# Stick-breaking attention layer: one copy of queries, keys and values out of PSUM, sums of squares and output halves off VectorE, keys converted first

## The chip, the core and the metric

The kernel runs on one core of a Trainium2 chip. The core has five engines that run their own instruction streams and meet at semaphores: TensorE (PE in the profile, its weight loads PEld), VectorE (DVE), ScalarE (ACT), GpSimd (POOL) and SyncE (SP), which issues the DMAs. The metric is the device time of one execution in microseconds (us), taken as the median of several runs. Lower is better.

## The reference

One step of a two-layer decoder trunk, in float32, for 1024 prompt rows and 64 sample rows (8 sequences of 8). Layer 0 is gated linear attention; layer 1, which the change touches, is stick-breaking attention with 16 heads of 64 columns:

```
u = rms_norm(x) @ w_in_b                      # 1024 -> 4 * 1024: q, k, v, gate
q, k = rms_norm(q per head) * qn, rms_norm(k per head) * kn
z = q . k / 8 + bias
a[t, s] = sigmoid(z[t, s]) * prod over s < j < t of (1 - sigmoid(z[t, j])),  s < t
y = x + ((a @ v) * silu(gate)) @ w_out_b      # k and v rows are outputs as well
```

## The kernel before

Matrix products run as float32r in three passes: each operand is split into a high part (a rounded copy) and a low part (the rest), and high·high, high·low and low·high are added up in PSUM. The rounded copy is an ACT activation, or a VectorE cast, and the rest is a subtraction on VectorE or POOL; for the weights these are `whi` (L219 on ACT, L221 on DVE) and `wlo` (L222).

Layer 1 runs over eight pairs of heads. For a pair PE makes nine blocks of rows (eight of 128 prompt rows, one of the 64 sample rows): `columns` multiplies the block's normalized rows by 384 columns of the weights (q, k and v of two heads) into a PSUM bank named `acc`, with 24 matmuls (L293). After every second block `gates` computes the gate columns for 256 rows, transposed, into an `acc` bank too (L315). The attention of the previous step runs between these matmuls: per step m (four to a pair) and head it goes over blocks of 256 keys. One unit is: logits `z` (four matmuls, L881), two sigmoids `om` and `A` on ACT (L884, L885), two running products `run` on DVE (scans, L904 on the diagonal, L907 elsewhere), a product `A` times `run` (L912, L915), transposes of `A` on PE (L928), their split into `aT` high (ACT L930) and low (DVE L931), and the matmuls with the values (L942). POOL hands the last column of one running product to the next (L899).

The steps around the change, by their functions:

- `qk_sums` takes a block's `acc` bank: ACT squares q and k of four heads (L799) and copies v out (L801), DVE adds the squares up per head (L802), POOL raises the mean to the power -0.5 (L804). For the sample block the bank is first copied to an SBUF tile `xr` (`whole_rows`).
- `qk_scale` multiplies q and k, still in the `acc` bank, by that factor (DVE L810); only then is the bank free for the next `columns` or `gates`. POOL makes the key output (L812); `v_parts` (L819, L820) splits the values.
- `qk_p` takes the blocks two by two: PE transposes q and k into a `tr` bank (L829), ACT and DVE split them into `qh`, `ql` and `kc`. The `tr` bank also serves the transposes of `A`.
- `gate_b` adds, at the end of a step, the two partial products of each head from the `o` bank (L952, L953) and multiplies by the gate (POOL L954); `store_b` sends the result to DRAM, or for the last pair to `H`, the input of the last projection.

PSUM has eight banks here, two each of `acc`, `tr`, `z` and `o`. PE's order is written out: every matmul has a due time (`at(...)`), and PE takes them by due time. The order on the other engines is made when the program is built, by a scheduler that plans with its own costs; each engine then works strictly in its order. Where ACT and DVE read the same PSUM bank, the built program puts a wait between them, so that one is done before the other starts.

Of the kernel before, what the change touches and what calls it, by code (L numbers as in the profile page):

```python
# [9 lines left out]
F32 = mybir.dt.float32  # L10
# [21 lines left out]
EPS = 1e-6  # L32
# [44 lines left out]
def tile_hybrid_decoder(ctx, tc, x_prompt, x_sample, state_gla, cache_k, cache_v, page_table,  # L77
# [16 lines left out]


    FIRST0, FIRST, FIRST5, RAW0 = 0.9, 1.5, 6, 0.9
    ACT_FROM, WHI, DLO = 90, 6, 3

    GAIN, CONSTS, SUP, LATE = -64.9, 2.5, 0.9, 9
    LAT, LAT0, LQ, LK = .7, 1.2, 1.4, 1.3  # L100
# [33 lines left out]
    def rows(t):  # L134
        return 128 if t < NP else NS
# [633 lines left out]
    def l1_consts():  # L769
        opened("keep")  # L770
        opened("at1")
        qn = K1["qn"] = const.tile([128, 1], F32, name="qn")
        for j in range(2):
            nc.sync.dma_start(qn[j * 64:(j + 1) * 64], cut(qnorm_b, 0, [[1, 64], [1, 1]]))
        nc.vector.tensor_scalar(qn, qn, DH ** -0.5, None, op0=OP.mult)
        bcast(K1.setdefault("kn", const.tile([128, DH], F32, name="kn")), knorm_b, 0, DH)
        knt = K1["knt"] = const.tile([128, 1], F32, name="knt")
        for j in range(2):
            nc.sync.dma_start(knt[j * 64:(j + 1) * 64], cut(knorm_b, 0, [[1, 64], [1, 1]]))
        bias = K1["bias"] = const.tile([128, 2, SH], F32, name="bias")  # L780
        bcast(bias[:, 0], sb_bias, 0, SH)
        nc.vector.tensor_scalar(bias[:, 1], bias[:, 0], -1.0, None, op0=OP.mult)
        gains = K1["gains"] = const.tile([128, 1], F32, name="gains")
        nc.vector.tensor_mul(gains, qn, knt)
        for name in ("qTs", "kTs", "gTs"):
            K1[name] = sb("keep", name, [128, PAIRS, NS], F32, 1)

        K1["sq"] = sb("at1", "sq", [128, 4, DH + 1], F32, 1)
        nc.gpsimd.memset(K1["sq"][:, :, DH:], EPS)

    def qk_sums(st, p, t):
        n = rows(t)
        if t == NP:
            whole_rows(st, "at1", 384)
        ps = st["ps"]
        sq = K1["sq"]
        q4 = ps[:n, :256].rearrange("p (h d) -> p h d", d=DH)
        ms = small.tile([128, 4], F32, name="ms4")
        nc.scalar.activation(sq[:n, :, :DH], q4, AF.Square, scale=1.0 / 8.0)  # L799
        st["v"] = sb("at1", "v", [128, 128])  # L800
        nc.scalar.activation(st["v"][:n], ps[:n, 256:384], AF.Copy)  # L801
        nc.vector.tensor_reduce(ms[:n], sq[:n], axis=AX.X, op=OP.add)  # L802
        st["rs"] = small.tile([128, 4], F32, name="rs4")
        nc.gpsimd.tensor_tensor(st["rs"][:n], ms[:n], half_exp[:n], op=OP.pow)  # L804

    def qk_scale(st, p, t):
        n, ps, rs = rows(t), st["ps"], st["rs"]
        q4 = ps[:n, :256].rearrange("p (h d) -> p h d", d=DH)
        qk = st["qk"] = sb("at1", "qk", [128, 4, DH], F32, 4)
        nc.vector.tensor_mul(qk[:n], q4, rs[:n, :, None].to_broadcast([n, 4, DH]))  # L810
        st["kout"] = sb("at1", "kout", [128, 2, DH])
        nc.gpsimd.tensor_mul(st["kout"][:n], qk[:n, 2:], K1["kn"][:n, None].to_broadcast([n, 2, DH]))  # L812

# [23 lines left out]
    def qk_p(sts, pair):  # L837

        tr = psum.tile([128, 4, 128], F32, name="tr")
        for x, st in enumerate(sts):
            turn_qk(st, 128, tr, (x, 2 + x))
        tr = tr.rearrange("p a s -> p (a s)")
        qp, kp, g = tr[:, :256], tr[:, 256:], K1["gains"]
        qh, kc = sb("at2", "qh", [128, 2, 256], F32R, NQ), sb("at2", "kc", [128, 2, 256], F32R, NKV)
        ql = K1["ql"][K1["turn"] % NQ]
        K1["turn"] += 1
        pair["q"].append((qh, ql))
        pair["k"].append(kc)  # L850
        up, dn = slice(0, 64), slice(64, 128)
        for dst, j, src in ((up, 0, up), (dn, 1, dn), (dn, 0, up), (up, 1, dn)):
            nc.scalar.activation(qh[dst, j], qp[src], AF.Copy, scale=g[src])  # L853
        nc.scalar.activation(kc[up, 0], kp[up], AF.Copy)
        nc.scalar.activation(kc[dn, 1], kp[dn], AF.Copy)
        nc.vector.scalar_tensor_tensor(ql[up, 0], qp[up], g[up], qh[up, 0], op0=OP.mult, op1=OP.subtract)
        nc.vector.scalar_tensor_tensor(ql[dn, 1], qp[dn], g[dn], qh[dn, 1], op0=OP.mult, op1=OP.subtract)
        nc.vector.tensor_sub(kc[dn, 0], kp[up], kc[up, 0])  # L858
        nc.vector.tensor_sub(kc[up, 1], kp[dn], kc[dn, 1])  # L859

    def gate_t(st, p, m, pair):
        ps, gt = st["ps"], sb("at1", "gt", [128, 256], F32, NG)
# [83 lines left out]
    def gate_b(q, pair, p, m):  # L946
        po = q["po"]
        sh, og = sb("at2", "sh", [128, 256], F32, 1), sb("at2", "og", [128, 256], F32, 2)
        q["og"] = og
        for j in range(2):  # L950
            main, other = slice(64 * j, 64 * j + 64), slice(64 - 64 * j, 128 - 64 * j)
            nc.scalar.activation(sh[main], po[other, j], AF.Copy)  # L952
            nc.vector.tensor_add(og[main], po[main, j], sh[main])  # L953
        nc.gpsimd.tensor_mul(og, og, pair["g"][m])  # L954

    def tps(m):
# [297 lines left out]
```

## Time and profile before

| | |
|---|---|
| median of three runs | 1348.04 us (1348.0 to 1350.47) |
| the profiled execution, its own time | 1349.09 us |
| its span, first to last instruction | 1347.4 us |
| granted TensorE clock | 1.00 over the whole span |
| busy, share of the span | PE 94%, PEld 84%, DVE 75%, ACT 53%, POOL 38% |
| layer 1's attention, 540 to 1210 us | eight pairs, one every 85 us |

A matmul's busy time overlaps the next one's, since they are pipelined: a stream of 384-column matmuls starts one every 0.17 to 0.18 us, though each is listed with 0.35 us. ACT's instructions overlap a little as well. "Idle before" and the list of waits count gaps that were ended by a semaphore, with the instruction that set it.

### The profile page before, as it was taken

The numbers are of one execution on the slowest core, as the hardware profiler recorded it, in microseconds if no ns is written. First come the engines' busy times: TensorE is split into PE (matmuls) and PEld (weight loads), VectorE is DVE, ScalarE is ACT, GpSimd is POOL, SyncE is SP. The second block draws the span as 40 slices with busy tenths as digits, with TensorE's granted clock in tenths as the row PEclk, the third lists the DMA queues.
The fourth block names the chain that finished last, engine by engine and source line by source line (L and its number), as shares of the span: only waits on it lengthen the run. The fifth ranks groups of instructions, "written<-read, shape, count | busy, mean of one in ns | idle before, by whom it ended". The sixth has DMA issues, their size and how long they took to land.

```text
span 1347.4 us, 23358 instructions
## 1 busy us (share of the span) xinstructions
PE 1269.9 (94%) x8025; PEld 1128.5 (84%) x8025; DVE 1011.1 (75%) x2047; ACT 708.4 (53%) x1640; POOL 515.5 (38%) x847
## 2 busy tenths in 40 slices
PE   6899999999999999989989999899998999999998
PEld 5788888888887787889989899898898998978665
DVE  7857858759565357698898988988889889896543
ACT  6446245254352034566666766667667677763221
POOL 6222323223222215363453734646446464443000
PEclk9999999999999999999999999999999999999999
DMA  6311402403327443020120200202002022134862
GB/s 193 91 41 44 135 20 59 124 17 100 121 90 240 135 137 117 20 73 27 34 71 23 71 27 28 79 23 70 28 28 77 21 78 86 33 124 152 316 204 79
DMA packets 118456, 115.80 MB, mean 86 GB/s; under 512 B 11002, under 2 KB 97922, under 8 KB 118338
## 3 DMA queue, kind: packets, MB, share of 16 engines
q1 hardware_dynamic: 118338, 114.31, 27.5%
q8 instruction: 64, 1.05, 0.3%
q14 instruction: 54, 0.44, 0.1%
HBM read 83.61 MB, written 30.67 MB: 85 GB/s over the span
## 4 chain that ended last, share of the span: by engine, by line
PE 56%; DVE 25%; ACT 7%; issue 5%; POOL 4%; DMA 3%; SPq 0%; DVEq 0%; POOLq 0%; ACTq 0%
PE acc L293 33%; PE acc L315 6%; DVE run L907 4%; PE z L881 3%; PE tr L928 3%; PE o L942 2%; DVE aT L931 2%; DVE whi L221 2%; ACT qh L853 2%; DVE qk L810 1%; POOL rs L804 1%; DVE A L912 1%; DVE A L915 1%; PE o L544 1%; DVE run L904 1%
## 5 line engine op out<-in xcount | busy, mean ns | idle before, releaser
L293 PE MATMUL acc<-whi,h 128*128 128x512 f32 (+1 forms) x1728 | 538.1, 374 | 9.3 <-DVE qk L810 6.2
L293 PEld LDWEIGHTS acc<-whi,h 128*128 128x128 f32 x1728 | 312.8, 189 | 40.3 <-ACT sh L952 3.8
L293 PE MATMUL acc<-wlo,h 128*128 128x512 f32 (+1 forms) x864 | 322.6, 373 | 3.9 <-DVE wlo L222 2.5
L315 PE MATMUL acc<-h,whi 128*128 128x256 f32 (+5 forms) x832 | 191.7, 316 | 19.1 <-DVE qk L810 8.7
L222 POOL TENSOR_TENSOR wlo<-wr,whi 128x512 fp32r<-128x512 f32 x98 | 144.4, 1478 | 127.4 <-DVE whi L221 92.5
L293 PEld LDWEIGHTS acc<-wlo,h 128*128 128x128 f32 x864 | 162.5, 188 | 22.1 <-DVE wlo L222 3.2
L315 PEld LDWEIGHTS acc<-h,whi 128*128 128x128 f32 (+2 forms) x832 | 137.8, 185 | 26.2 <-issue 10.6
L907 DVE TENSOR_TENSOR_SCAN run<-om,run 128x256 f32<-128x256 f32 x192 | 141.8, 779 | 15.6 <-ACT om L884 15.1
L930 ACT ACTIVATE aT<-tr 128x512 fp32r<-128x512 f32 (+1 forms) x160 | 89.0, 556 | 82.8 <-PE tr L928 80.9
L884 ACT ACTIVATE om<-z,bias 128x512 f32<-128x512 f32 (+1 forms) x160 | 103.1, 644 | 48.3 <-PE z L881 39.6
L293 PE MATMUL acc<-w,h 128*128 128x384 f32 (+1 forms) x480 | 122.0, 365 | 0.8 <-DVE qk L810 0.8
L315 PE MATMUL acc<-h,wlo 128*128 128x256 f32 (+2 forms) x392 | 122.2, 312 | 0.3 <-POOL wlo L222 0.3
L931 DVE TENSOR_TENSOR aT<-tr,aT 128x512 fp32r<-128x512 f32 (+1 forms) x160 | 100.9, 631 | 9.7 <-ACT aT L930 7.4
L928 PE MATMUL tr<-ident,A 128*128 128x128 f32 x576 | 90.0, 274 | 18.6 <-DVE kc L859 8.4
L885 ACT ACTIVATE A<-z,bias 128x512 f32<-128x512 f32 (+1 forms) x160 | 102.4, 640 | 0.0
L942 PE MATMUL o<-aT,v 128*128 128x256 f32 (+1 forms) x640 | 98.1, 274 | 0.0
L928 PEld LDWEIGHTS tr<-ident,A 128*128 128x128 f32 x576 | 68.9, 140 | 34.0 <-ACT sq L799 9.0
L942 PEld LDWEIGHTS o<-aT,v 128*128 128x128 f32 x640 | 94.4, 188 | 1.7 <-DVE aT L931 1.0
L804 POOL TENSOR_TENSOR rs<-ms,half_exp 128x4 f32<-128x4 f32 (+1 forms) x72 | 86.2, 1198 | 21.3 <-DVE ms L802 18.8
L881 PE MATMUL z<-kc,qh 128*128 128x256 f32 x320 | 84.4, 286 | 7.2 <-DVE kc L858 7.2
L293 PEld LDWEIGHTS acc<-w,h 128*128 128x128 f32 x480 | 83.2, 189 | 6.3 <-issue 0.8
L899 POOL COPY run<-run 128x2 f32<-128x2 f32 x96 | 32.8, 342 | 135.7 <-DVE run L907 78.1
(273 smaller groups left out, 2488.7 us busy)
## 6 DMA issues: line engine op xcount, KB each, us to landing
wr<-in_w_in_b_dram SPq DMA_DIRECT2D x64, 256.0 KB, 3.0
wr<-in_w_in_a_dram SPq DMA_DIRECT2D x32, 256.0 KB, 2.9
kp<-in_cache_k_dram SPq DMA_DIRECT2D x16, 512.0 KB, 4.6
vp<-in_cache_v_dram SPq DMA_DIRECT2D x16, 512.0 KB, 4.9
o_d<-og SPq DMA_DIRECT2D x60, 128.0 KB, 1.8
x<-in_x_prompt_dram SPq DMA_DIRECT2D x8, 512.0 KB, 5.2
wr<-in_w_in_a_dram SPq DMA_DIRECT2D x32, 128.0 KB, 3.9
n<-in_state_gla_dram SPq DMA_DIRECT2D x8, 512.0 KB, 4.2
```

Source lines behind the costliest of these rows:

```text
L222: engine.tensor_sub(e.lo[:, :m], raw[:, :m], e.hi[:, :m])
L293: nc.tensor.matmul(st["ps"][:x.shape[1], :n], x, (w[k].hi if part == 0 else w[k].lo)[:, :n], start=first, stop=last)
L315: nc.tensor.matmul(st[key][:x.shape[1], :n], x, y, start=first, stop=last)
L804: nc.gpsimd.tensor_tensor(st["rs"][:n], ms[:n], half_exp[:n], op=OP.pow)
L881: nc.tensor.matmul(out, lhs, rhs, start=x == 0, stop=x == len(mm) - 1)
L884: nc.scalar.activation(u["om"][:, v0:], z[:, v0:], AF.Sigmoid, scale=-1.0, bias=K1["bias"][:, 1, hd:hd + 1])
L885: nc.scalar.activation(u["A"][:, v0:], z[:, v0:], AF.Sigmoid, bias=K1["bias"][:, 0, hd:hd + 1])
L907: nc.vector.tensor_tensor_scan(run[:, a, n - 1::-1], rev, rev, before[:, a, 0:1], op0=OP.mult, op1=OP.bypass)
L928: nc.tensor.transpose(tr[:, x], u["A"][:, col:col + 128], ident)
L930: nc.scalar.activation(hi[:, v0:], tr[:, v0:], AF.Copy)
L931: nc.vector.tensor_sub(lo[:, v0:], tr[:, v0:], hi[:, v0:])
L942: nc.tensor.matmul(q["po"][:, j, q0:], vs, part[:, x * 256 + q0:(x + 1) * 256], start=first and n == 0, stop=last and n == 3)
```

## The change

It is in layer 1, and in which engine rounds some of its weights.

- `qk_sums`: ACT copies the whole `acc` bank, 384 columns, to an SBUF tile `qkv` (L797). The four heads' squares are taken from that tile, one activation per head with the sum as an accumulated output (L801, four times). The sum on DVE is gone. POOL's power takes a helper with two instructions, an addition of the small constant and the power (L248, L249).
- `qk_scale` multiplies in place in `qkv` (DVE L807), reading two SBUF tensors, where it read PSUM and one SBUF tensor.
- `qk_p`: the same splits in another order, keys first, each high part followed by its low part. The second copies of the high queries are made from the SBUF tile (L858, L859).
- `gate_b`: ACT copies both halves out of the `o` bank (four copies, L952 and L953), POOL adds them (L954).
- `WHI` goes from 6 to 8: of each eight weight tiles whose first use comes after a due time of 90, all are rounded on ACT (L219), not six.

```diff
-    ACT_FROM, WHI, DLO = 90, 6, 3
+    ACT_FROM, WHI, DLO = 90, 8, 3
...
-        K1["sq"] = sb("at1", "sq", [128, 4, DH + 1], F32, 1)
-        nc.gpsimd.memset(K1["sq"][:, :, DH:], EPS)
+        K1["sq"] = sb("at1", "sq", [128, 4, DH], F32, 1)
...
         ps = st["ps"]
         sq = K1["sq"]
-        q4 = ps[:n, :256].rearrange("p (h d) -> p h d", d=DH)
+
+        all3 = sb("at1", "qkv", [128, 384], F32, 4)
+        nc.scalar.activation(all3[:n], ps[:n, :384], AF.Copy)
+        st["qk"], st["v"] = all3[:, :256].rearrange("p (h d) -> p h d", d=DH), all3[:, 256:]
         ms = small.tile([128, 4], F32, name="ms4")
-        nc.scalar.activation(sq[:n, :, :DH], q4, AF.Square, scale=1.0 / 8.0)
-        st["v"] = sb("at1", "v", [128, 128])
-        nc.scalar.activation(st["v"][:n], ps[:n, 256:384], AF.Copy)
-        nc.vector.tensor_reduce(ms[:n], sq[:n], axis=AX.X, op=OP.add)
+        for h in range(4):
+            nc.scalar.activation(sq[:n, h], st["qk"][:n][:, h], AF.Square, scale=1.0 / 8.0, accum_out=ms[:n, h:h + 1])
         st["rs"] = small.tile([128, 4], F32, name="rs4")
-        nc.gpsimd.tensor_tensor(st["rs"][:n], ms[:n], half_exp[:n], op=OP.pow)
+        rsqrt(st["rs"][:n], ms[:n])
 
     def qk_scale(st, p, t):
-        n, ps, rs = rows(t), st["ps"], st["rs"]
-        q4 = ps[:n, :256].rearrange("p (h d) -> p h d", d=DH)
-        qk = st["qk"] = sb("at1", "qk", [128, 4, DH], F32, 4)
-        nc.vector.tensor_mul(qk[:n], q4, rs[:n, :, None].to_broadcast([n, 4, DH]))
+        n, rs, qk = rows(t), st["rs"], st["qk"]
+        nc.vector.tensor_mul(qk[:n], qk[:n], rs[:n, :, None].to_broadcast([n, 4, DH]))
...
         up, dn = slice(0, 64), slice(64, 128)
-        for dst, j, src in ((up, 0, up), (dn, 1, dn), (dn, 0, up), (up, 1, dn)):
-            nc.scalar.activation(qh[dst, j], qp[src], AF.Copy, scale=g[src])
         nc.scalar.activation(kc[up, 0], kp[up], AF.Copy)
+        nc.vector.tensor_sub(kc[dn, 0], kp[up], kc[up, 0])
         nc.scalar.activation(kc[dn, 1], kp[dn], AF.Copy)
+        nc.vector.tensor_sub(kc[up, 1], kp[dn], kc[dn, 1])
+        nc.scalar.activation(qh[up, 0], qp[up], AF.Copy, scale=g[up])
         nc.vector.scalar_tensor_tensor(ql[up, 0], qp[up], g[up], qh[up, 0], op0=OP.mult, op1=OP.subtract)
+        nc.scalar.activation(qh[dn, 1], qp[dn], AF.Copy, scale=g[dn])
         nc.vector.scalar_tensor_tensor(ql[dn, 1], qp[dn], g[dn], qh[dn, 1], op0=OP.mult, op1=OP.subtract)
-        nc.vector.tensor_sub(kc[dn, 0], kp[up], kc[up, 0])
-        nc.vector.tensor_sub(kc[up, 1], kp[dn], kc[dn, 1])
+
+        nc.scalar.activation(qh[dn, 0], qh[up, 0], AF.Copy)
+        nc.scalar.activation(qh[up, 1], qh[dn, 1], AF.Copy)
...
         q["og"] = og
         for j in range(2):
             main, other = slice(64 * j, 64 * j + 64), slice(64 - 64 * j, 128 - 64 * j)
+            nc.scalar.activation(og[main], po[main, j], AF.Copy)
             nc.scalar.activation(sh[main], po[other, j], AF.Copy)
-            nc.vector.tensor_add(og[main], po[main, j], sh[main])
+        nc.gpsimd.tensor_add(og, og, sh)
         nc.gpsimd.tensor_mul(og, og, pair["g"][m])
```

PE's order does not change: its matmuls stand in the same sequence. What changes there are waits. At the gates of step 0 of the fifth pair (`acc` banks with their numbers) PE has before:

```order
L293 MATMUL acc_10235<-w0103_10058,h1_81 128x384
L293 MATMUL acc_10235<-whi_10071,h0_80 128x384
L293 MATMUL acc_10235<-wlo_10072,h0_80 128x384
L293 MATMUL acc_10235<-whi_10071,h1_81 128x384
L315 MATMUL acc_10327<-h0_80,whi_8903 128x256 [waits DVE_49,PE_49]
L315 MATMUL acc_10327<-h1_81,whi_8903 128x256
```

And with the change:

```order
L293 MATMUL acc_10320<-w0103_10141,h1_81 128x384
L293 MATMUL acc_10320<-whi_10154,h0_80 128x384
L293 MATMUL acc_10320<-wlo_10155,h0_80 128x384
L293 MATMUL acc_10320<-whi_10154,h1_81 128x384
L315 MATMUL acc_10414<-h0_80,whi_8964 128x256
L315 MATMUL acc_10414<-h1_81,whi_8964 128x256
```

The first gate matmul's wait on DVE (for L810, which freed its bank) is gone; an earlier wait of PE covers what remains.

On ACT, at the third conversion of the fourth pair (`kc` and `qh` are the converted keys and queries, `aT` the transposed weights of an attention unit, `sq` the squares), the order before is:

```order
L885 ACTIVATE A<-z,bias 128x512
L853 ACTIVATE qh<-tr,gains 64x256 [waits PE_49]
L853 ACTIVATE qh<-tr,gains 64x256 x3
L854 ACTIVATE kc<-tr 64x256
L855 ACTIVATE kc<-tr 64x256
L930 ACTIVATE aT_9855<-tr 128x384 [waits PE_49,Activation_49]
L799 ACTIVATE sq<-acc 128x4x64 [waits PE_49]
L801 ACTIVATE v<-acc 128x128 [waits DMAHW7_49]
```

With the change:

```order
L885 ACTIVATE A<-z,bias 128x512
L849 ACTIVATE kc<-tr 64x256 [waits PE_49]
L851 ACTIVATE kc<-tr 64x256 [waits DVE_49]
L930 ACTIVATE aT_9933<-tr 128x384 [waits PE_49,Activation_49]
L797 ACTIVATE qkv<-acc 128x384 [waits DMAHW3_49,PE_49]
L853 ACTIVATE qh<-tr,gains 64x256 [waits DVE_49]
L801 ACTIVATE sq,ms_9950<-qkv 128x64 [waits Activation_49]
L801 ACTIVATE sq,ms_9950<-qkv 128x64 x3
L858 ACTIVATE qh<-qh 64x256 [waits Activation_49]
L855 ACTIVATE qh<-tr,gains 64x256 [waits DVE_49]
L859 ACTIVATE qh<-qh 64x256 [waits Activation_49]
```

Six activations in a row have become a sequence with three waits on DVE in it, and with other work between them.

On DVE, at the same conversion (`ql` is the low part of the queries), before:

```order
L915 TENSOR_TENSOR A<-A,run 128x512 [waits DVE_49,Activation_49,Pool_49]
L856 SCALAR_TENSOR_TENSOR ql_5789<-tr,gains,qh 64x256 [waits PE_49,Activation_49]
L857 SCALAR_TENSOR_TENSOR ql_5789<-tr,gains,qh 64x256
L858 TENSOR_TENSOR kc<-tr,kc 64x256
L859 TENSOR_TENSOR kc<-tr,kc 64x256
L931 TENSOR_TENSOR aT_9856<-tr,aT_9855 128x384 [waits Activation_49]
```

With the change:

```order
L915 TENSOR_TENSOR A<-A,run 128x512 [waits DVE_49,Activation_49,Pool_49]
L850 TENSOR_TENSOR kc<-tr,kc 64x256 [waits Activation_49]
L852 TENSOR_TENSOR kc<-tr,kc 64x256 [waits Activation_49]
L931 TENSOR_TENSOR aT_9934<-tr,aT_9933 128x384 [waits Activation_49]
L854 SCALAR_TENSOR_TENSOR ql_5791<-tr,gains,qh 64x256 [waits Activation_49]
L856 SCALAR_TENSOR_TENSOR ql_5791<-tr,gains,qh 64x256 [waits Activation_49]
L807 TENSOR_TENSOR qkv<-qkv,rs_9955 128x256 [waits DMAHW3_49,Pool_49]
```

One wait on ACT has become four, each for one activation, and the scaling L807 stands in this stretch with a wait on POOL.

## Rows read from the trace of the kernel before

**Rows 1.** Layer 1: length, busy us of PE, PEld, DVE, ACT, POOL; clock, DMA

```profile
540.00:1210.00 670.00, 625.87 (x4335) 595.43 (x4336) 581.12 (x1114) 453.57 (x965) 337.65 (x570) 1.00 0.17 51
```

**Rows 2.** The chain that ended last, by engine, whole span

```profile
PE 56%; DVE 25%; ACT 7%; issue 5%; POOL 4%; DMA 3%; SPq 0%; DVEq 0%; POOLq 0%; ACTq 0%
```

**Rows 3.** PE's waits, 540 to 1210 us: total, times, longest

```profile
PE acc L315 <- DVE qk L810: 10.4, 7, 1.7
PE tr L928 <- DVE kc L859: 8.4, 6, 2.4
PE z L881 <- DVE kc L858: 7.2, 10, 1.4
PE acc L293 <- DVE qk L810: 7.0, 14, 1.2
PE tr L928 <- ACT sq L799: 4.5, 7, 1.0
```

**Rows 4.** Timeline, 852 to 860 us: start, length, instruction [idle before <- releaser]

```profile
852.21 0.39 ACT L799 ACTIVATE sq<-acc 128x256 f32<-128x256 f32 x1 [1.25 <-DVE ms L802]
...
854.55 0.42 DVE L802 TENSOR_REDUCE ms<-sq 128x4 f32<-128x260 f32 x1
...
856.17 1.38 POOL L804 TENSOR_TENSOR rs<-ms,half_exp 128x4 f32<-128x4 f32 x1
...
859.54 0.41 DVE L810 TENSOR_TENSOR qk<-acc,rs 128x256 f32<-128x256 f32 x1
...
860.10 0.36 PE L315 MATMUL acc<-h,whi 128*128 128x256 f32 x1 [1.72 <-DVE qk L810]
```

**Rows 5.** Groups by shape, 540 to 1210 us: count | busy us, mean ns | idle

```profile
L930 ACT ACTIVATE aT<-tr 128x384 fp32r<-128x384 f32 x63 | 30.9, 491 | 43.7 <-PE tr L928 43.3
L953 DVE TENSOR_TENSOR og<-o,sh 64x256 f32<-64x256 f32 x62 | 25.7, 415 | 1.7
L952 ACT ACTIVATE sh<-o 64x256 f32<-64x256 f32 x62 | 23.5, 379 | 35.9 <-DVE og L953 34.9
L801 ACT ACTIVATE v<-acc 128x128 f32<-128x128 f32 x61 | 17.4, 285 | 0.0
L221 DVE CAST whi<-wr 128x512 fp32r<-128x512 f32 x14 | 9.4, 669 | 0.0
```

**Rows 6.** Groups by shape on POOL, whole span

```profile
L954 POOL TENSOR_TENSOR og<-og,gt 128x256 f32<-128x256 f32 x32 | 26.6, 830 | 37.9 <-DVE og L953 37.9
L248 POOL TENSOR_SCALAR ms<-ms 128x1 f32<-128x1 f32 x32 | 8.5, 267 | 119.2 <-ACT og L645 118.8
```

**Rows 7.** ACT's timeline in layer 0, 173 to 176 us

```profile
173.81 0.40 ACT L561 ACTIVATE qh<-g 128x64 fp32r<-128x64 f32 x2
174.24 0.39 ACT L645 ACTIVATE og<-o 128x256 f32<-128x256 f32 x1
174.52 0.20 ACT L645 ACTIVATION_READ_ACCUMULATOR og<-o 128x1 f32 x1
174.61 0.38 ACT L529 ACTIVATE gt<-acc 128x256 f32<-128x256 f32 x1
```

**Rows 8.** Timeline, 822.5 to 829.5 us: the fourth pair's third conversion

```profile
822.59 0.60 PE L829 MATMUL tr<-ident,qk 128*128 128x128 f32 x4
...
823.23 1.92 ACT L853 ACTIVATE qh<-tr,gains 64x256 fp32r<-64x256 f32 x4
...
824.62 0.49 PE L928 MATMUL tr<-ident,A 128*128 128x128 f32 x3
...
826.97 0.42 DVE L858 TENSOR_TENSOR kc<-tr,kc 64x256 fp32r<-64x256 f32 x1
...
827.53 0.36 PE L881 MATMUL z<-kc,qh 128*128 128x256 f32 x1 [0.56 <-DVE kc L858]
```

**Rows 9.** DVE's and POOL's timelines, 854 to 857 us

```profile
854.88 1.18 DVE L810 TENSOR_TENSOR qk<-xr,rs 64x256 f32<-64x256 f32 x1
...
854.38 1.39 POOL L222 TENSOR_TENSOR wlo<-wr,whi 128x512 fp32r<-128x512 f32 x1
```

## Prediction

> **What bounds the kernel now.** I read the busy times of layer 1 first, since the change is only there: of 670 us PE is busy for 626, DVE 581, ACT 454 and POOL 338 [rows 1]. So PE sets the pace, and what a change of waits can give back is at most its idle time, 670 - 625.9 = 44 us. Next the chain of waits: 56% of the span on PE, 25% on DVE, only 7% on ACT and 4% on POOL [rows 2]. PE's fixed order stops now and then, and mostly DVE lets it go on. Then the list of PE's waits, to see for what: five rows make 37.5 of the 44 us [rows 3]. They are of two families. In the first, a new product needs an `acc` bank that L810 has not yet read: 10.4 + 7.0 = 17.4 us. In the second, PE waits for the conversion of keys and queries, either for the first logits (7.2 us, L858) or for the `tr` bank that the conversion still reads (8.4 us, L859, and 4.5 us which the view puts down to L799, at the first conversion of each pair). Last I read one wait of each family in the timeline [rows 4, 8].
>
> **The change, part by part.**
>
> *The copy out of PSUM.* The timeline shows what held the bank: the block is complete at 852.2, ACT squares it at once, but DVE adds up at 854.55, POOL's power starts at 856.17, L810 at 859.54, and PE, which had come to its gates at 860.10 - 1.72 = 858.4, goes on at 860.10 [rows 4]. With the change the bank is free when the copy L797 ends. For its time I take ACT's copy of the same shape out of PSUM, 0.49 us [rows 5]. The bank would be free near 852.7, some 5 us before PE wants it, which covers an ACT that is late. So the first family goes: -17.4 us. What is late next is the scaling itself: L807 still waits for POOL, and on DVE scans or a product of `A` stand behind it, for which PE's transposes wait. If that gives back all of the gate waits, the L315 row, -7.0 us is left; this is the other end.
>
> *The conversion, in another order.* Six activations and then four DVE operations become eight steps in turn, because the engines may not read the bank together; L851, L853 and L855 each wait for DVE, and behind them on ACT stand the copies L930 and the sigmoids L884 that PE needs. For the first logits I add up the new order at the third conversion, where PE waited 0.56 us before [rows 8]. The transposes end at 823.2. L849 0.38, L850 0.42, L851 0.38 bring 824.4 (before, the same activations and subtractions took 0.38 and 0.42 [rows 5, 8]); L930 must wait for its transposes, which end at 825.1, and takes 0.49; then L797 0.49, L853 0.48 (a quarter of 1.92 [rows 8]), the four squares 0.96 (below), L858 0.4: 827.9. With hand-offs it is 828.0, against 827.53. The logits of one head need no more than this, as its low query part L854 is done by then. So 0.5 us is lost per pair, times 8: +4 us. The ends: -7.2 us if the wait vanishes, and, if two DVE steps take 1.18 us, as L810 beside POOL [rows 9], in place of 0.42, 0.5 + 2 x 0.76 = 2.0 us per pair, +16 us.
>
> The wait for the `tr` bank, 8.4 + 4.5 = 12.9 us, does not stay as it is: by the built program's semaphores the transposes that waited for L859 now take the other bank at most conversions and wait for the L931 that read it. That operation comes early in the conversion, but with one bank left the units follow one another more strictly. I take half, -6.5 us; the ends are -12.9 and, were the wait twice as long, +12.9.
>
> *Loads.* DVE loses 72 sums of 0.42 us [rows 4], 64 additions of 0.415 and 16 casts of 0.67 [rows 5]: 30.2 + 26.6 + 10.7 = 67.5 us. L807 is another instruction than L810: it reads two SBUF tensors. Out of PSUM L810 takes 0.41 us [rows 4]; its sample form, which reads two SBUF tensors as well, took 1.18 us while POOL ran, and ended 0.29 us after POOL's instruction [rows 9]. So 64 of them cost between nothing and 64 x 0.77 = 49 us more; POOL is busy half of the time [rows 1], so I take 25. DVE then has 581 - 67.5 + 25 = 539 us.
>
> ACT gains most. A 64-column activation adds 0.15 us (two in 0.40, one alone 0.25), and an accumulated output 0.09 (the next instruction starts that long after the read of the accumulator) [rows 7]: 0.24 per square, 0.96 for four. With the copy, 0.52, that is 1.48 us, against 0.39 + 0.285 less 0.1 of overlap for L799 and L801 [rows 4, 5]: +0.9, times 72, +65 us. At most, with nothing overlapped, a square costs 0.25 + 0.20, and this is +125. To it come 64 more copies in `gate_b` of 0.38 us [rows 5], +24, and the 16 casts, +11. ACT has 454 + 100 = 554 us, at most 614. POOL gains 72 additions of about 0.27 and 32 sums of 0.83 us [rows 6], 19 + 27: 384 us.
>
> All three stay below PE's 626 and lie beside it, so the loads themselves cost nothing in my sum; what they cost if that cover is too thin is in the rivals. In `gate_b` the work from the `o` bank to the result grows from two copies and two additions in turn (1.6 us) to four copies and a sum on POOL (2.35 us). Only the last step of the last pair has the next stage waiting for it: +0.8 us.
>
> *Sum.* The profiled execution's own time is 1349.1 us (span 1347.4), 1 us above the median of the runs: 1349.1 - 17.4 + 4.0 - 6.5 + 0.8 = 1330.0, and 1329 on the scale of the median.
>
> **Rivals.**
>
> *Hand-offs between ACT and DVE become the bound (slower).* The place is `qk_p`: ACT, now at 83 to 92% load, stands still at L851, L853 and L855 until DVE has finished scans queued ahead of its part. The price is the upper end of both conversion terms: 12.9 + 16 + 0.8 - 17.4 = +12.3, or 1361 us. It decides from the point where a pair loses more than the 2.2 us (17.4 over 8) that the free banks give it: logits of the third conversion later than 4.9 + 2.2 = 7.1 us after its transposes start, against 4.9 before. For it speak the three new waits. Against it: before the change ACT took up the conversion 0.04 us after the transposes [rows 8], so it had no queue.
>
> *VectorE is not lightened (no change).* L807 pays 49 us, and POOL's 46 us more hold DVE's scans and products, which read two SBUF tensors too, for two fifths of that time, 18 us: DVE is at 581 - 67.5 + 67 = 581 again. The chain's 25% on DVE stays, and what the banks give PE returns as waits for `A` and `aT`: 1349 us. The 1.18 us of [rows 9] speak for it; against it, that the two waits of L810 needed no faster DVE to go, only an earlier release. The Trainium skill has this as a rule (GPSIMD Engine Reference, section Key points): GpSimd shares its SBUF interfaces with VectorE and contends with VectorE instructions that have two SBUF inputs. The trace agrees, with 1.18 against 0.41 us. By that rule this rival is the outcome if POOL is nearly always at work when L807 starts.
>
> *Everything goes (faster still).* If both families vanish, 17.4 + 12.9 + 7.2 = 37.5 us of the 44 are won: 1312 us. An ACT without a queue and a DVE with 40 us less speak for it; that PE would then run 40 us ahead of engines at over 80% load speaks against it.
>
> **How the numbers follow.** The forecast (1312 to 1346 us by its own terms) has a chance of 0.50, the last rival 0.14, no change 0.14, slower 0.22. A measurement of this kernel can tell 0.2%, 2.7 us, from no change. The rival without change lies within that with 0.08, on the faster side with 0.05 and on the slower with 0.01. Faster: 0.50 + 0.14 + 0.05 = 0.69; same 0.08; slower 0.22 + 0.01 = 0.23. The range reaches from just below the lowest sum, 1310, into the slower rival, 1357.
>
> **What would show it.** Right: the rows for `acc` that name L810 are gone from PE's waits, with none for L807 and only tenths for L797 in their place; DVE near 540 us and ACT near 550 in layer 1; squares of 0.25 us, starting 0.24 apart; L807 between 0.4 and 1.2 us, long where POOL is busy; L881 of a third conversion some 5.4 us after its transposes start. The forecast is wrong if PE's idle time in layer 1 does not fall by some 20 us: with ACT rows (`aT`, `kc`, `qh`) on top of PE's waits the first rival holds, with `A` or `aT` on DVE and L807 near 1.2 us the second.

## The result, and the profile after

The changed kernel takes 1359.74 us (median of four runs, 1357.2 to 1363.18) against 1348.02 us before (median of four): a ratio of 1.0083, 95% interval 1.0067 to 1.0098. It is slower by 0.8%; the forecast was 1329 us, with a range of 1310 to 1357. The profiled execution's own time is 1363.18 us, 14.1 above the profiled one of before, and 3.4 above the median of its runs, which matters when its numbers are added up.

The busy times of layer 1 after, columns as in [rows 1]; the window is 10 us longer, since the same work now takes about that much more:

```profile
540.00:1220.00 680.00, 632.54 (x4341) 608.11 (x4340) 530.37 (x971) 532.21 (x1537) 378.74 (x673) 0.98 0.17 50
```

The engines are loaded as intended: DVE fell from 581 to 530 us, ACT rose from 454 to 532. But PE's idle time did not fall from its 44 us. It is 680 - 632.5 = 47.5, and PE's own busy time grew by 6.7 us at a mean clock of 0.98 where it was 1.00. So of 10 us lost here 3.4 are idle and 6.7 are slower matmuls; the other 4 are lost mostly at layer 1's first transposes and, 3.4 of them, in the sample stage.

The chain that ended last, after (before: [rows 2]):

```profile
PE 49%; DVE 22%; ACT 14%; POOL 7%; issue 5%; DMA 2%; DVEq 0%; SPq 0%; POOLq 0%; ACTq 0%
```

ACT's share doubled, PE's fell by 7 points. PE's waits after, the same view and window as [rows 3]:

```profile
PE tr L928 <- DVE aT L931: 19.0, 19, 1.9
PE z L881 <- ACT qh L858: 16.8, 8, 2.7
PE tr L928 <- DVE A L915: 4.8, 7, 1.2
PE o L942 <- DVE aT L931: 4.2, 4, 1.2
PE z L881 <- DVE ql L854: 2.7, 1, 2.7
```

Both `acc` rows, 17.4 us, are gone and nothing named L797 or L807 took their place. In their stead stand 19.5 us for first logits (7.2 before), 23.8 for the `tr` bank (12.9 before in the two rows of [rows 3], 17.5 in all its rows) and 4.2 for `aT` at L942. The timeline shows how, at the third conversion of the fourth pair, the place of [rows 8]; here it is the pair before, where nothing differs but the start (start, length, instruction, [idle before <- releaser]):

```profile
737.27 0.60 PE L826 MATMUL tr<-ident,qkv 128*128 128x128 f32 x4
...
737.95 0.38 ACT L849 ACTIVATE kc<-tr 64x256 fp32r<-64x256 f32 x1
...
738.24 1.74 DVE L907 TENSOR_TENSOR_SCAN run<-om,run 128x256 f32<-128x256 f32 x2
...
740.11 0.69 DVE L915 TENSOR_TENSOR A<-A,run 128x512 f32<-128x512 f32 x1
...
740.84 0.42 DVE L850 TENSOR_TENSOR kc<-tr,kc 64x256 fp32r<-64x256 f32 x1
...
741.29 0.38 ACT L851 ACTIVATE kc<-tr 64x256 fp32r<-64x256 f32 x1 [2.96 <-DVE kc L850]
741.69 0.49 ACT L930 ACTIVATE aT<-tr 128x384 fp32r<-128x384 f32 x1
...
742.08 0.48 ACT L797 ACTIVATE qkv<-acc 128x384 f32<-128x384 f32 x1
...
742.45 0.46 ACT L853 ACTIVATE qh<-tr,gains 64x256 fp32r<-64x256 f32 x1
...
742.81 0.25 ACT L801 ACTIVATE sq<-qkv 128x64 f32<-128x64 f32 x1
...
743.89 0.41 ACT L858 ACTIVATE qh<-qh 64x256 fp32r<-64x256 f32 x1
...
744.36 0.38 PE L881 MATMUL z<-kc,qh 128*128 128x256 f32 x1 [2.68 <-ACT qh L858]
```

ACT begins at once, and then stands for 2.96 us, because DVE's half L850 is queued behind a pair of scans and a product. The copy and the four squares come between L851 and L858. The logits start 7.1 us after the transposes; before it was 4.9.

What the clock did there, by windows (columns as in [rows 1]; the third number from the end is the granted clock):

```profile
740.00:745.30 5.30, 2.62 (x18) 2.29 (x18) 3.04 (x6) 3.88 (x16) 2.14 (x6) 1.00 0.05 16
745.30:748.70 3.40, 3.40 (x15) 3.31 (x15) 2.96 (x7) 1.63 (x3) 0.65 (x2) 0.50 0.08 24
748.70:752.10 3.40, 3.40 (x25) 3.40 (x25) 0.84 (x2) 1.57 (x3) 0.00 (x0) 1.00 0.00 0
```

PE was busy for half of 5.3 us; then the granted clock is 0.50, the lower of its two levels, 1.2 GHz, for 3.4 us with PE full, and 15 matmuls are done where the next 3.4 us at 2.4 GHz do 25.

PE's order is the same before and after, so each matmul can be set beside its twin. By this the changed kernel loses 3.7 us at that conversion, 2.1 at the logits and 1.6 under the low clock, but wins most of that back within the pair: it is 1.3 us behind the kernel before at the second pair's first conversion, level at the fourth's third, 4.3 behind at the seventh's first and 5.8 at the last pair's first. The other 8.3 of 14.1 us are lost from there on, where the clock falls for 6.8 us in the last pair and once more in the sample stage.

### The profile page after: what moved, and what is told of

It reads as the page before. It is cut to its first block, busy times and chain, and to the rows that moved or that the text cites. A ratio compares the mean times of both kernels' runs of the same rounds, so it can differ in the third digit from the quotient of the medians.

```text
span 1361.5 us, 23619 instructions
## 1 busy us (share of the span) xinstructions
PE 1276.3 (94%) x8025; PEld 1140.7 (84%) x8025; DVE 957.0 (70%) x1895; ACT 788.6 (58%) x2224; POOL 558.5 (41%) x950
## 4 chain that ended last, share of the span: by engine, by line
PE 49%; DVE 22%; ACT 14%; POOL 7%; issue 5%; DMA 2%; DVEq 0%; SPq 0%; POOLq 0%; ACTq 0%
PE acc L293 31%; PE acc L315 5%; DVE run L907 5%; POOL rs L249 2%; ACT sq L801 2%; PE z L881 2%; DVE A L915 2%; PE o L942 2%; DVE aT L931 2%; ACT aT L930 2%; PE tr L928 2%; ACT om L884 1%; DVE whi L221 1%; PE o L544 1%; PE tr L1109 1%
## 5 line engine op out<-in xcount | busy, mean ns | idle before, releaser
L222 POOL TENSOR_TENSOR wlo<-wr,whi 128x512 fp32r<-128x512 f32 x98 | 137.4, 1410 | 120.7 <-DVE whi L221 89.7
L907 DVE TENSOR_TENSOR_SCAN run<-om,run 128x256 f32<-128x256 f32 x192 | 146.5, 803 | 30.6 <-ACT om L884 29.9
L931 DVE TENSOR_TENSOR aT<-tr,aT 128x512 fp32r<-128x512 f32 (+1 forms) x160 | 101.3, 633 | 55.5 <-ACT aT L930 54.1
L928 PE MATMUL tr<-ident,A 128*128 128x128 f32 x576 | 92.9, 281 | 23.8 <-DVE aT L931 19.0
L249 POOL TENSOR_TENSOR rs<-ms,half_exp 128x4 f32<-128x4 f32 (+3 forms) x108 | 105.3, 975 | 8.9
L930 ACT ACTIVATE aT<-tr 128x512 fp32r<-128x512 f32 (+1 forms) x160 | 88.2, 551 | 31.5 <-PE tr L928 29.9
L881 PE MATMUL z<-kc,qh 128*128 128x256 f32 x320 | 85.7, 289 | 19.5 <-ACT qh L858 16.8
L942 PE MATMUL o<-aT,v 128*128 128x256 f32 (+1 forms) x640 | 99.9, 277 | 4.2 <-DVE aT L931 4.2
L928 PEld LDWEIGHTS tr<-ident,A 128*128 128x128 f32 x576 | 72.0, 144 | 37.5 <-DVE aT L931 24.5
L942 PEld LDWEIGHTS o<-aT,v 128*128 128x128 f32 x640 | 96.5, 192 | 6.1 <-DVE aT L931 5.5
L248 POOL TENSOR_SCALAR ms<-ms 128x4 f32<-128x4 f32 (+3 forms) x108 | 33.0, 305 | 155.6 <-ACT og L645 125.8
```

The lines of the kernel that those rows point to most:

```text
L222: engine.tensor_sub(e.lo[:, :m], raw[:, :m], e.hi[:, :m])
L249: nc.gpsimd.tensor_tensor(dst, mean, half_exp[:mean.shape[0], :mean.shape[1]], op=OP.pow)
L881: nc.tensor.matmul(out, lhs, rhs, start=x == 0, stop=x == len(mm) - 1)
L907: nc.vector.tensor_tensor_scan(run[:, a, n - 1::-1], rev, rev, before[:, a, 0:1], op0=OP.mult, op1=OP.bypass)
L928: nc.tensor.transpose(tr[:, x], u["A"][:, col:col + 128], ident)
L930: nc.scalar.activation(hi[:, v0:], tr[:, v0:], AF.Copy)
```

## The experiments

All were timed beside the kernel before, in five rounds. Its median there was 1348.7 to 1349.8 us; the changed kernel was not timed again, so differences to it are good to some 2 us.

### The changed kernel in the old order of the halves

```
+        for dst, j, src in ((up, 0, up), (dn, 1, dn), (dn, 0, up), (up, 1, dn)):
+            nc.scalar.activation(qh[dst, j], qp[src], AF.Copy, scale=g[src])
         nc.scalar.activation(kc[up, 0], kp[up], AF.Copy)
-        nc.vector.tensor_sub(kc[dn, 0], kp[up], kc[up, 0])
         nc.scalar.activation(kc[dn, 1], kp[dn], AF.Copy)
...
```

> The changed kernel with the conversion in qk_p as it was before: six activations, then four VectorE operations; all other parts of the change stay. Theory (the hand-offs between ACT and DVE in the conversion cost the time): PE's wait for the first logits of the third conversion falls from 2.7 us to about the 0.6 us of before, the granted clock stays at 1.00 in layer 1, the waits for acc stay away; 1325 to 1338 us. Rival (ACT, with the squares, the copies and the gate halves, is too slow and is what PE waits for): the waits for aT and A stay, ACT has only lost nothing, and the time stays above 1352 us.

1345.28 us, ratio 0.9964 (0.9951 to 0.9978). The order costs 14 us in this kernel. But everything else together wins 4.5 us at most, where the forecast had 17.4 for the banks alone; the range I expected was missed. Set beside their twins, its matmuls win 9.5 us from the second pair's first conversion to the seventh's, and 5.7 are lost ahead of these and behind them. Some of its waits in layer 1:

```profile
PE tr L925 <- DVE kc L856: 10.0, 11, 2.6
PE tr L925 <- DVE A L909: 7.3, 6, 1.3
...
PE tr L826 <- DVE kTs L832: 6.0, 7, 1.6
```

The second and the last are new: transposes, next in PE's order, wait for DVE's product and for the sample block's keys.

### Only the order changed

```
-        for dst, j, src in ((up, 0, up), (dn, 1, dn), (dn, 0, up), (up, 1, dn)):
-            nc.scalar.activation(qh[dst, j], qp[src], AF.Copy, scale=g[src])
         nc.scalar.activation(kc[up, 0], kp[up], AF.Copy)
+        nc.vector.tensor_sub(kc[dn, 0], kp[up], kc[up, 0])
         nc.scalar.activation(kc[dn, 1], kp[dn], AF.Copy)
...
```

> The kernel before with the new order in qk_p alone. Theory of the hand-offs: PE's waits for L810 stay at about 17 us, the wait at the third conversion grows to 2.5 to 3.5 us per pair, the granted clock drops for some us after it; 1365 to 1385 us. Rival (ACT's load): ACT has hardly more to do than before, so 1345 to 1351 us.

1350.33 us, ratio 1.0007 (0.9998 to 1.0016). By itself the order costs nothing that can be measured; I had expected the whole loss. Its third conversion in the timeline:

```profile
733.70 0.38 ACT L852 ACTIVATE kc<-tr 64x256 fp32r<-64x256 f32 x1
...
735.77 0.38 ACT L854 ACTIVATE kc<-tr 64x256 fp32r<-64x256 f32 x1 [1.69 <-DVE kc L853]
...
736.98 0.46 ACT L856 ACTIVATE qh<-tr,gains 64x256 fp32r<-64x256 f32 x1
...
737.48 0.41 ACT L861 ACTIVATE qh<-qh 64x256 fp32r<-64x256 f32 x1
...
737.95 0.38 PE L884 MATMUL z<-kc,qh 128*128 128x256 f32 x1 [0.49 <-ACT qh L861]
```

The hand-off is there, but DVE is late by 1.69 us and not 2.96, and the query half and its copy start 0.50 apart and not 1.44, since no squares stand between them. The two differences are 1.3 and 0.9 us, together the 2.2 us by which the changed kernel's logits are later.

### The same steps, grouped by engine

```
         nc.scalar.activation(kc[up, 0], kp[up], AF.Copy)
-        nc.vector.tensor_sub(kc[dn, 0], kp[up], kc[up, 0])
         nc.scalar.activation(kc[dn, 1], kp[dn], AF.Copy)
-        nc.vector.tensor_sub(kc[up, 1], kp[dn], kc[dn, 1])
         nc.scalar.activation(qh[up, 0], qp[up], AF.Copy, scale=g[up])
-        nc.vector.scalar_tensor_tensor(ql[up, 0], qp[up], g[up], qh[up, 0], op0=OP.mult, op1=OP.subtract)
         nc.scalar.activation(qh[dn, 1], qp[dn], AF.Copy, scale=g[dn])
+        nc.vector.tensor_sub(kc[dn, 0], kp[up], kc[up, 0])
+        nc.vector.scalar_tensor_tensor(ql[up, 0], qp[up], g[up], qh[up, 0], op0=OP.mult, op1=OP.subtract)
+        nc.vector.tensor_sub(kc[up, 1], kp[dn], kc[dn, 1])
...
```

> The changed kernel with the conversion grouped: the four activations that read PSUM first (keys, then queries), the two copies of the queries from SBUF behind them, then the four VectorE operations in a row. Theory of the hand-offs: the bank is read by ACT for 1.7 us in place of 2.7 us before, DVE waits once, so the third conversion's logits wait for less than 0.6 us and the time is 1 to 8 us below the run with the old order, 1320 to 1335 us. Rival (ACT's load): within 3 us of the changed kernel, about 1360 us.

1335.29 us, ratio 0.9899 (0.9884 to 0.9915): 24 us below the changed kernel and 14 below the kernel before. It is at the upper edge of the range expected, but 10 us below the old order, more than the 1 to 8 expected. There is one hand-off now. The third conversion:

```profile
733.83 0.38 ACT L849 ACTIVATE kc<-tr 64x256 fp32r<-64x256 f32 x1 [0.15 <-PE tr L826]
...
735.60 0.42 ACT L857 ACTIVATE qh<-qh 64x256 fp32r<-64x256 f32 x1
735.61 0.42 DVE L853 TENSOR_TENSOR kc<-tr,kc 64x256 fp32r<-64x256 f32 x1 [0.25 <-ACT qh L852]
```

ACT goes through without a wait; DVE, coming late from the same scans, is late once. PE's waits for first logits fell from 19.5 us to 0.3.

### The changed kernel with PE kept busy

```
+            if m == 2 and diag and j == 0 and p < PAIRS - 1:
+                for x in range(12):
+                    nc.tensor.matmul(z[:, :384], H[0][:, x % NK, :128], H[0][:, x % NK, 128:512], start=True, stop=True)
```

> The changed kernel with twelve more matmuls of 384 columns (2.1 us, into the z bank, overwritten by the logits) just before the first logits of step 2 in each pair but the last, where PE stands idle 2.7 us. Theory (the granted clock falls to half for 3.4 us because PE stood still): PE's idle time there falls to some 0.6 us, the clock stays at 1.00 after it, and about 1.5 us per pair is won although PE does more: 1347 to 1353 us. Rival (the clock falls for another cause, or the fall costs nothing because PE waits anyway): clock still 0.988 to 0.99, 1358 to 1364 us; if the twelve matmuls lengthen the path, above that.

1350.9 us (11 runs), ratio 1.0010 (0.9999 to 1.0021). Twelve matmuls are added ahead of the logits that come late (which overwrite what they leave in the `z` bank), and the time falls by 9 us. PE's timeline there:

```profile
741.69 2.25 PE L876 MATMUL z<-h 128*128 128x384 f32 x12
744.54 0.39 PE L884 MATMUL z<-kc,qh 128*128 128x256 f32 x1 [0.59 <-ACT qh L858]
```

The logits come as late as before the filling (744.54 and 744.36), only the clock behind them stays at 1.00. Over the whole run the mean granted clock is 0.996 where it was 0.989 (means of all runs). So some 9 of the 11.7 us are the fall of the clock after PE's standstills, as was expected. They are not won evenly: set beside their twins, the matmuls of the two kernels lie level at the fourth pair's third conversion, 5.8 us apart at the seventh's and 8.7 at the end.

### One Square and VectorE's sum, in the changed order

```
...
-        for h in range(4):
-            nc.scalar.activation(sq[:n, h], st["qk"][:n][:, h], AF.Square, scale=1.0 / 8.0, accum_out=ms[:n, h:h + 1])
+        nc.scalar.activation(sq[:n, :, :DH], st["qk"][:n], AF.Square, scale=1.0 / 8.0)
+        nc.vector.tensor_reduce(ms[:n], sq[:n], axis=AX.X, op=OP.add)
         st["rs"] = small.tile([128, 4], F32, name="rs4")
-        rsqrt(st["rs"][:n], ms[:n])
+        nc.gpsimd.tensor_tensor(st["rs"][:n], ms[:n], half_exp[:n], op=OP.pow)
```

GpSimd's addition ahead of the power goes with the four squares, as before the change.

> The changed kernel, but with one Square over all four heads (from the copied rows) and the VectorE sum of before in place of the four accumulating squares; keys-first order, one copy and gate as changed. Theory A: the order costs 14 us only together with the four squares, which stand 0.96 us on ScalarE between the first query half and its copy (L853 742.45, L858 743.89). One Square of about 0.4 us there brings the first logits of the third conversion from 7.1 to about 6.5 us after their transposes, PE's wait for it from 2.7 to about 2.1, and the fall of the granted clock goes with it: 1341 to 1351, z waits 9 to 12 us. Theory B: VectorE's lateness (the scan pair beside GpSimd's sum, 1.27 us) is what counts: 1355 to 1362, z waits 15 to 19, since VectorE gets 0.41 us more in each sum.

1339.81 us, ratio 0.9938 (0.9925 to 0.9952), 20 us below the changed kernel. ACT at the third conversion (its transposes start at 731.37, PE's logits at 736.79, 5.4 us):

```profile
735.53 0.46 ACT L854 ACTIVATE qh<-tr,gains 64x256 fp32r<-64x256 f32 x1
735.89 0.41 ACT L801 ACTIVATE sq<-qkv 128x256 f32<-128x256 f32 x1
736.32 0.41 ACT L859 ACTIVATE qh<-qh 64x256 fp32r<-64x256 f32 x1
```

0.65 us is won between the query half and its copy (0.79 for 1.44), and DVE's first key half starts 1.92 us after ACT's and not 2.89. The clock no longer falls behind the logits. The z waits are 11.4 us, as Theory A expected, and Theory B falls; but of the 1.7 us by which the logits come earlier Theory A had only the 0.65. The other 0.97 are DVE's, which is less late here although it has more to do, and the gain is somewhat more than expected.

### The old gate, in the changed order

```
-            nc.scalar.activation(og[main], po[main, j], AF.Copy)
             nc.scalar.activation(sh[main], po[other, j], AF.Copy)
-        nc.gpsimd.tensor_add(og, og, sh)
+            nc.vector.tensor_add(og[main], po[main, j], sh[main])
```

> The changed kernel with the output halves summed as before (two copies on ScalarE, two sums on VectorE). Theory B: the scan pair took 1.74 us beside GpSimd's sum and product of the outputs where it takes 1.39 without, and the whole chain of VectorE ran 1.27 us later than with the order alone; without the GpSimd sum the first logits come 0.4 to 1.3 us sooner, z waits fall from 16.8 to 7 to 13, the clock stays up: 1344 to 1353. Theory A (squares between the halves) alone: z waits stay at 15 to 18 and the time within 3 us of 1359.7.

1373.99 us, ratio 1.0182 (1.0168 to 1.0196). Both expectations missed, on the other side. The copy and the sum of `gate_b` are a hand-off as well:

```profile
738.10 0.60 PE L826 MATMUL tr<-ident,qkv 128*128 128x128 f32 x4
...
738.75 0.38 ACT L952 ACTIVATE sh<-o 64x256 f32<-64x256 f32 x1 [1.89 <-DVE og L953]
...
740.40 1.39 DVE L907 TENSOR_TENSOR_SCAN run<-om,run 128x256 f32<-128x256 f32 x2
...
740.79 0.37 ACT L849 ACTIVATE kc<-tr 64x256 fp32r<-64x256 f32 x1
```

The scans are back at 1.39 us without GpSimd beside them, but ACT, held by DVE's sum, begins the conversion 2.7 us after its transposes, and the logits come 8.1 us after them. Moving the sums off DVE was thus a part of the change that helped, in this order.

### Only the one copy and the four squares

```
+        nc.scalar.activation(all3[:n], ps[:n, :384], AF.Copy)
+        for h in range(4):
+            nc.scalar.activation(sq[:n, h], st["qk"][:n][:, h], AF.Square, scale=1.0 / 8.0, accum_out=ms[:n, h:h + 1])
...
```

> The kernel before with only the one copy of queries, keys and values out of the accumulator and the four accumulating squares on ScalarE (old order of the halves, old gate, old share of conversions on ScalarE). Forecast of the prediction: 17.4 us of accumulator waits go and nothing comes back: 1329 to 1333. Theory C: of each 1.88 us won at the gate's accumulator 1.47 come back at the next transposes, which wait for VectorE's product, and the block behind the sample keys waits for the next bank: 1340 to 1346, about as the changed kernel in the old order (1345.3).

1352.78 us, ratio 1.0029 (1.0016 to 1.0041): slower, and by more than either theory allowed. (The scaling in SBUF and GpSimd's addition come with the copy and the squares.) Matched matmul by matmul with the kernel before, most pairs win 1.88 us at the gates, 0.40 and 0.74 at later blocks, and lose 1.8 to 1.9 at the block behind the sample rows, 0.68 at the third conversion and some tenths behind it. The row that takes most of it back:

```profile
PE tr L826 <- DVE kTs L832: 12.7, 7, 2.6
```

What is left is 3.8 us won in the five pairs from the second's first conversion to the seventh's. The loss lies at the layer's start, in the last pair and in the sample stage, and the granted clock falls to 0.50 for 3.4 us there four times (at 539.3, 1123.0, 1204.9 and 1252.7 us), as it never does in the trace of the kernel before but at its very end.

### The grouped order with the old gate

The diffs of the grouped order and of the old gate together.

> The grouped order (four halves from the bank in a row on ScalarE, then the two copies; 1335.3 with the changed gate) with the output halves summed as before. If VectorE's product before the transposes is what still waits (8.3 + 6.0 us), two sums of 0.42 us more on VectorE for each output make it slower: 1337 to 1342. If GpSimd's sum beside VectorE's scans is the dearer one: 1328 to 1334.

1334.41 us, ratio 0.9897 (0.9882 to 0.9912). Just above the second expectation, and the same as with the changed gate (1335.29). What cost 14 us in the order of many hand-offs costs nothing in the order of one.

### The grouped order with one Square

The diffs of the grouped order and of the one Square together.

> The grouped order (1335.3 with four squares) with one Square over all four heads and VectorE's sum of before. Theory: one Square shortens the way from the accumulator to the reciprocal roots by 0.5 us on ScalarE and 0.3 us on GpSimd, so the transposes behind the sample rows wait for the sample keys no longer (5.9 us in the grouped kernel, 0.2 in the kernel with one Square and the changed order), and the transposes after the third conversion wait less (6.9 us): 1324 to 1331. Rival: with the hand-offs gone the four squares cost nothing any more, and 0.41 us more on VectorE in each sum make it 1334 to 1340.

1319.19 us (1317.66 to 1320.46), ratio 0.9773 (0.976 to 0.9786), lower than expected; it beats the kernel before by 30.5 us and the changed one by 40. One Square instead of four is worth 16 us in this order too, so the rival falls; the wait for the sample keys went from 5.9 to 0.6 us, as the theory had it. Its layer 1 and its first waits:

```profile
540.00:1210.00 670.00, 649.38 (x4500) 622.55 (x4499) 582.56 (x1076) 504.25 (x1064) 377.16 (x619) 1.00 0.19 56
```

```profile
PE tr L928 <- DVE A L912: 8.0, 6, 1.4
PE tr L928 <- DVE A L915: 5.5, 7, 1.9
```

PE idles for 20.6 us of 670. VectorE has 583 us, as much as before the change [rows 1], and the kernel is 30 us faster: it was not VectorE's load that had to go down.

### The same with the old gate

> The same with the output halves summed on VectorE as before, so that against the kernel before only the one copy, the grouped order and the share of conversions on ScalarE differ. With four squares the gate made no difference in the grouped order (1335.3 and 1334.4). Theory: none here either, within 3 us of the kernel with the changed gate. Rival: VectorE now carries sums of squares and outputs again (some 33 us more than in the changed kernel) and binds: 4 to 10 us slower than it.

1320.85 us, ratio 0.979 (0.9776 to 0.9803), 1.7 above the kernel with the changed gate, with DVE at 600 us in 670. The gate makes no difference here either, as expected.

### Only the gate changed

> The kernel before with only the output halves changed (both copied on ScalarE, summed on GpSimd). The prediction put it at +0.8 us at the end and nothing elsewhere: 1347 to 1351. Rival: since in the changed order the old gate cost 14.2 us, the changed gate may be worth as much alone: 1335 to 1343, with the waits for VectorE's products and key halves (7 to 9 us each) shorter.

1351.54 us, ratio 1.0019 (1.0009 to 1.0028): +1.8 us, just above the range of the prediction's +0.8. The rival falls.

### Only the share of the weights' conversions changed

```
-    ACT_FROM, WHI, DLO = 90, 6, 3
+    ACT_FROM, WHI, DLO = 90, 8, 3
```

> The kernel before with only the share of the raw weights' conversions on ScalarE changed (all eight of eight where six were). The prediction put it at no cost: 1346 to 1350. Rival: the conversions stand on ScalarE ahead of sigmoids or squares and make PE wait for them: 1351 to 1356. The four parts alone would then sum to what the whole change did (+11.7 us) or, by the theory that they cost only together, to much less.

1343.65 us, ratio 0.9959 (0.9945 to 0.9973): 6.1 us faster, which neither side expected. The timeline shows a part of it, at the last conversion of the fourth pair; before, and then here:

```profile
840.61 0.96 DVE L221 CAST w<-wr 128x512 fp32r<-128x512 f32 x1
...
841.72 1.27 POOL L222 TENSOR_TENSOR w<-wr,w 128x512 fp32r<-128x512 f32 x1 [0.43 <-DVE w L221]
842.09 2.81 DVE L904 TENSOR_TENSOR_SCAN run<-om,eye 128x128 f32<-128x128 f32 x2
...
847.35 0.52 PE L928 MATMUL tr<-ident,A 128*128 128x128 f32 x3 [1.17 <-DVE kc L859]
```

```profile
837.06 2.04 DVE L904 TENSOR_TENSOR_SCAN run<-om,eye 128x128 f32<-128x128 f32 x2
...
841.83 0.52 PE L928 MATMUL tr<-ident,A 128*128 128x128 f32 x3
```

Before, DVE's cast stood ahead of the two scans, which began 1.8 us after the transposes of the conversion (840.31); here they begin 0.65 us after them (836.41). Before, GpSimd's subtraction also began just ahead of the scans, and they took 2.81 us; here one begins with them, and they take 2.04. PE's 1.17 us for L859 behind them are gone. PE's wait for L859 fell from 8.4 us [rows 3] to 1.4.

Alone, the four parts come to +4.0 + 0.6 + 1.8 - 6.1 = +0.3 us, each good to 1 or 2 us; together they are +11.7. The loss is in their meeting.

## Why the prediction was wrong

**The banks (-17.4).** Right as a mechanism: the rows are gone. As a gain it did not last. In the kernel with only the copy the gates' 1.88 us and some more are won in most pairs, and nearly all comes back within the same pair, mostly as waits for the sample keys: 0.8 us a pair is left (3.8 in five), not 2.2. I had let the late scaling give back the gates' 10.4 us at the worst, with 7.0 still won, and looked for it at the product of `A` alone.

**The first logits (+4).** This is the step that failed: "L849 0.38, L850 0.42, L851 0.38 bring 824.4". It lets DVE begin L850 when ACT has ended L849. On DVE, L850 stood behind two scans and a product, and started 2.89 us after L849, not 0.38. I had checked ACT's queue only ("it had no queue"). DVE's could be read in the trace of before, in the stretch of [rows 8]:

```profile
822.59 1.40 DVE L907 TENSOR_TENSOR_SCAN run<-om,run 128x256 f32<-128x256 f32 x2 [0.22 <-ACT om L884]
...
824.12 0.69 DVE L915 TENSOR_TENSOR A<-A,run 128x512 f32<-128x512 f32 x1
...
825.97 0.48 DVE L856 SCALAR_TENSOR_TENSOR ql<-tr,gains,qh 64x256 fp32r<-64x256 f32 x1 [1.16 <-ACT kc L855]
```

The product ends at 824.81, so L850 could not start at 823.6, where the sum has it, but 1.2 us later. The rest of the delay came with the change: the scans start 0.97 us after the transposes do (before, together with them) and take 1.74 us for 1.40. Before the change DVE's queue cost nothing here, since ACT went through its six activations meanwhile and DVE then waited 1.16 us for them. In the new order ACT waits for DVE in the middle, and what is queued on ACT (the copy and squares) is paid behind it. The term measured 19.5 - 7.2 = +12.3 us, near its upper end of 16.

**The `tr` bank (-6.5).** Wrong in sign. The term counted two of the four rows of L928 before; the others are:

```profile
PE tr L928 <- ACT A L885: 2.4, 2, 1.2
PE tr L928 <- DVE aT L931: 2.2, 8, 0.4
```

Like for like it is 23.8 against 17.5 us, +6.3. The cause is the same hand-off, now at the fourth conversion. In the third pair L851 again waits 2.96 us for DVE's L850, L930 stands on ACT behind L851, DVE's L931 behind L930, and PE's transposes wait 1.43 us for L931, where they had waited 1.20; at the next two units they wait 0.57 and 0.55 us, where they had not waited. With the order alone the row for `aT` is as high (19.5 us), so it belongs to the order, but there the first logits (4.2 us) and the `acc` bank (11.7) waited less in return. With all four rows of `acc` before (19.8 us) and the new one of L942, PE's waits changed by -19.8 + 12.3 + 6.3 + 4.2 = +3.0 us.

**The clock.** Not in the sum at all. The runs put about 9 us on it.

**Loads at no cost.** DVE at 530 and ACT at 532 us are near the 539 and 554 worked out. A square took 0.247 us and the next began 0.24 later, as worked out. But load was the wrong measure: four squares or one made 20 us of difference, with the lighter DVE in the slower kernel. (DVE's sum and GpSimd's addition changed along with the squares; their shares were not separated.) The gate's +0.8 was +1.8. That the casts' move gives nothing was wrong by 6.1 us, to the other side.

**The rivals.** The slower one held: place (`qk_p`), cause (ACT stands until DVE has finished scans queued ahead), threshold (logits at 7.1 us) and even the time, 1361 for 1359.7. Its price was put together from the ends of the conversion terms, 16 and 12.9 us, which measured 12.3 and 6.3, and it left out the clock, so that the agreement in the total is in good part luck. The rival of a VectorE not lightened falls, by the groups by shape after:

```profile
L807 DVE TENSOR_TENSOR qkv<-qkv,rs 128x256 f32<-128x256 f32 x62 | 27.7, 446 | 20.7 <-POOL rs L249 19.7
...
L807 DVE TENSOR_TENSOR qkv<-qkv,rs 64x256 f32<-64x256 f32 x8 | 9.2, 1149 | 0.1
```

L807 with two SBUF inputs took 0.45 us, 0.03 more than L810, not 1.18. The sample form's 1.15 is a mean of eight: 0.42 alone, 0.51 to 0.56 four times, and 2.23 three times, beside some 2.1 us of GpSimd work. The rule of the Trainium skill (GPSIMD Engine Reference, section Key points) that GpSimd contends with two-input VectorE work is seen in the scans: 1.74 us for the pair that overlaps GpSimd's product of the outputs, 1.39 where it does not. It is seen at L807 too, but there it is rare: 49 of the 64 run alone or beside nothing but a small copy or fill of GpSimd, in about 0.42 us, and only the seven beside GpSimd's sum of the output halves take 0.60 (seven beside a cast 0.50).

How much of the 9 us each single standstill costs, and how the first logits of the last pair came to wait for DVE's L854 (2.7 us), was not taken apart. Nor is it shown why the last pair and the sample stage lose 8.3 us; the order is not all of it, since the changed kernel in the old order loses 4.8 us there, and the one with only the copy 5.2.

## What to carry to other kernels

When two engines split one buffer and may not use it together, let each take all its parts in one go: every further hand-off makes an engine wait for whatever is queued ahead of its partner's part, and that has to be read in both engines' queues. Price an instruction that is moved to a less loaded engine by what stands behind it in that queue, not by its busy time. And a wait that is removed is won only if the next instruction in the bound engine's order was not waiting for the same late engine.

## What the runs showed of the hardware

After a wait of 2.68 us at the logits the granted clock fell from 1.00 to 0.50 for 3.4 us, while PE was full. In the changed kernel this happens behind the third conversion of five pairs (at 659.9, 745.3, 830.6, 915.9 and 1086.6 us, after waits of 2.38 to 2.68 us), for 6.8 us at 1175.4, and once more in the sample stage. Behind a wait of 2.40 us at 1001.88 it does not happen, nor behind one of 2.65 us in the kernel with one Square (at 1156.20), and in layer 1 of the kernel before, where one wait lasted 2.4 us too [rows 3], never. The waits alone do not settle it. A stop can cost PE more than its own length: behind the 2.68 us at 744.36 another 1.6 us were lost under the low clock, and twelve matmuls whose results nothing uses, put into the gap in seven pairs, bought 9 us.
